# Hybrid recurrent and sparse-attention trunk: a slot table of its own for the first layer

## Chip, cores and metric

The kernel runs on one core of a Trainium2 chip. The metric is the device time of one execution in microseconds (us). The kernel before took 248.72 us (median of 3 runs, 248.48 to 249.34).

## The reference

Two layers, each with one RMS norm, one combined input projection, two mixers in parallel and one output projection onto the residual. The input is 256 tokens of width 1024, all in 32-bit floats.

```python
h = rms_norm(x, norm_g)
z = h @ w_in            # rg_x, rg_gate, q, k_c, v_c, k_s, v_s, k_w, v_w, nsa_gate, br_gate
y_a = rg_lru(causal_depthwise_conv(rg_x, conv_w, conv_b), ...) * silu(rg_gate)
y_b = nsa(q, k_c, v_c, k_s, v_s, k_w, v_w, br_gate, ...) * silu(nsa_gate)
return x + concatenate([y_a, y_b]) @ w_out
```

Mixer A is a gated linear recurrence: two small block products of the convolved rg_x give the gates r and i (tanh forms), from them a decay a and an input u = sqrt(1 - a^2) * i * x, and a scan over the tokens. Mixer B is attention of 8 heads in 2 groups with three branches. The compressed branch turns overlapping blocks of 32 tokens of k_c and v_c through a two-layer network (first product, silu, second product) into 15 keys and values per group; its softmax is small. The selected and the sliding branch cover here the same causal keys. The three are mixed by gates and multiplied by a silu gate.

## The kernel before, in words

Each weight matrix comes in chunks of up to 128 x 1024. A chunk is split into a high part in a rounded format (`wh`) and the rest (`wl`, VectorE, line 170), and each product is three TensorE passes (lines 175 to 177). A layer has 13 chunks ahead of those that matter here (q, keys, compressor input, values), then 12 chunks of 8 x 3 products of 256 columns (function `fm`), which the program calls slots 0 to 11: x0 to x3 (input of the recurrence), n0, n1, g0 to g3, n2, n3 (silu gates of attention and recurrence). Slots 12 to 19 are the output projection (`out_proj`).

The other work of the layer is hung on the slots. The table `SL` says which step stands at which slot, and `at(n, f, ..., mid)` enters it: a step stands ahead of the slot's products, with `mid` after the DMA issues of the slot but still ahead of the products. The loop at the end (lines 842 to 859) writes the program in that order: steps of the slot, loads, casts, mid steps, products, the step that takes up the products (`rg_x`, `rg_gate`, `nsa_gate`), splits of the chunks to come.

That text is not yet the order on the engines. A planner makes one queue per engine out of it: it takes, in a model of the times, the instruction that stands earliest in the text among those whose inputs and buffers are there in the model. On the chip each engine then works through its queue in that fixed order. So a step that is not ready (in the model) is passed by later ones, and a slot's products fill in between.

The steps that the change touches:
- `qk_transpose(t)` (lines 366 to 387): transposes q and k of token block t; copies on ScalarE, rests on VectorE (line 385 writes `qs`), and a copy `qT` (line 387). The second block stands at slot 2 in layer 0, at slot 1 in layer 1.
- The compressor: `cmp_hid` (slot 1), `cmp_act` (slot 2; line 472 writes `hs` on VectorE), `cmp_kv` (second product, lines 477 and 478 on TensorE, a short ScalarE, GpSimd and VectorE chain behind it to line 495), `cmp_kt` (line 499), `cmp_scores` (line 511 and a softmax), `cmp_pt` (line 538).
- Attention for head pair i and token block t: `att_scores` (lines 581 to 583; maximum on VectorE, lines 586 or 588; exponentials on ScalarE, line 594), `att_coef` (ScalarE, line 609), `att_turn` (transposes, line 622, copied out by line 83). `att_out(0)` (lines 636 to 642, slot 7) takes the turned probabilities of head pairs 0 and 1 and the output of `cmp_pt`.
- `rg_gates(j)` (line 665 on TensorE, then lines 668, 669, 671 and 672 on ScalarE), `rg_sqrt` (line 681, ScalarE), `rg_scan` (slot 8).

PSUM banks: the products of `fm` and those of `rg_gates` share two banks (tag "fm"); a bank is free again when its reader has read it: lines 668 and 669 for a gate product, line 654 (VectorE, in `rg_x`) for an x slot, line 544 for a pair of silu slots. Scores have three banks (tag "s"), transposes two ("pp"), the compressor and `att_out` one ("m").

In layer 0 of the kernel before, slot 2 holds `qk_transpose(1)`, `cmp_act`, `att_coef(0,0)` and `rg_gates(0)`; slot 3 holds `cmp_kv`, `att_scores(0,1)`, `att_scores(1,0)`, `att_turn(0,0)` and `rg_gates(1)`, then the products of x3.

Of the kernel before, what the change touches and what calls it, by code (L numbers as in the profile page):

```python
# [38 lines left out]
for _n, _w in (("g", 8), ("cw", 16), ("cb", 4), ("br", 4), ("bi", 4), ("lam", 4)):  # L39
# [12 lines left out]
K = dict(scale="A", ev1="A", hid="A", pct="A")  # L52
SL = dict(qk=(0, 2), order=("x0", "x1", "x2", "x3", "n0", "n1", "g0", "g1", "g2", "g3", "n2", "n3"),
          cmp=(2, 3, 4), att=(1, 3, 3, 4, 6, 7, 10, 11), turn=(3, 4, 5, 6, 8, 10,
          12, 13), cs=(5, 5), cpt=6, aout=(7, 15), gates=(2, 3, 4, 5), tab=6, sqrt=5,
          scan=8, rout=(9, 11))

# [12 lines left out]
def hybrid_trunk_kernel(ctx: ExitStack, tc: tile.TileContext, vx, wc, wt, wv, wf, wo, w1, w2, pe,  # L72
# [185 lines left out]
    def layer(l, prev):  # L258
# [4 lines left out]
        def step(chunk, run, after=None, before=(), middle=()):  # L263
            steps.append((chunk, run, after, before, middle))
# [506 lines left out]
             [F(norm_rope, 1)] + ([] if l else [rms2]))  # L771
        step(Chunk(wv[l, 0, :, 3:6], 3, 280), R(tm2, 3, 3))
        step(Chunk(wv[l, 0, :, 6:], 2, 280), R(tm2, 6, 2), v_out)
        order = [(o[0], int(o[1])) for o in SL["order"]]
        base = {"x": 0, "g": 4, "n": 8}
        post = {"x": rg_x, "g": rg_gate, "n": nsa_gate}
        plan = [([], []) for _ in range(16)]
# [1 line left out]
        def at(n, f, *a, mid=False):  # L779
            plan[n][1 if mid else 0].append(F(f, *a))  # L780

        at(1, cmp_hid)
        at(SL["qk"][0], qk_transpose, 0)
        at(SL["qk"][1] - l, qk_transpose, 1)
        for n, f in zip(SL["cmp"], (cmp_act, cmp_kv, cmp_kt)):
            at(n, f)
        for q in range(8):
            i, t = divmod(q, 2)
            n = SL["att"][q]
            at(n, att_scores, i, t)  # L790
            if q == 0:
                at(SL["qk"][1] - l, att_coef, i, t, mid=bool(l))
            else:
                at(n, att_coef, i, t, mid=True)
        at(SL["cs"][0], cmp_scores)
        at(SL["cpt"], cmp_pt)
        for q in range(8):
            at(SL["turn"][q], att_turn, *divmod(q, 2))
        for i in range(4):
            if i < 2:  # L800
                at(SL["aout"][i], att_out, i)
            at(SL["gates"][i], rg_gates, i)
        at(SL["tab"], next_gains, mid=True)
        at(SL["sqrt"], rg_sqrt, mid=True)
        at(SL["scan"], rg_scan, mid=True)
        for i in range(2):
            at(SL["rout"][i], rg_out, 2 * i, mid=True)
        for n, (kind, j) in enumerate(order):
            c = Chunk(wf[l, base[kind] + j], KT, P, dma=n >= 4)

# [13 lines left out]
    for l in range(DEPTH):  # L824
        prev, st_ = layer(l, prev)
        prev0 = prev0 or prev
        steps += st_
# [140 lines left out]
```

## Time and profile before

| | |
|---|---|
| median of 3 runs | 248.72 us (248.48 to 249.34) |
| the profiled execution | 248.43 us, of which the span of its instructions 246.6 us |
| TensorE busy | 240.6 us (98%), weight loads 222.2 us (90%) |
| VectorE, ScalarE, GpSimd busy | 195.6, 163.8, 38.8 us |
| granted TensorE clock | 0.9 or more in all 40 slices of the page |
| DMA | 57.17 MB, 232 GB/s mean |

The span leaves 1.8 us of the execution outside the instructions. Busy shares overlap: an engine that is busy may be ahead of or behind the one that sets the end. A matmul row gives a start and a modelled end; since matmuls are pipelined, the cost of one is read from the distance between two starts (0.12 us for a product of 256 columns in a run of them).

### The profile page before, as it was taken

The numbers are of one execution on the slowest core, as the hardware profiler recorded it, in microseconds if no ns is written. First come the engines' busy times: TensorE is split into PE (matmuls) and PEld (weight loads), VectorE is DVE, ScalarE is ACT, GpSimd is POOL, SyncE is SP. The second block draws the span as 40 slices with busy tenths as digits, with TensorE's granted clock in tenths as the row PEclk, the third lists the DMA queues.
The fourth block names the chain that finished last, engine by engine and source line by source line (L and its number), as shares of the span: only waits on it lengthen the run. The fifth ranks groups of instructions, "written<-read, shape, count | busy, mean of one in ns | idle before, by whom it ended". The sixth has DMA issues, their size and how long they took to land.

```text
span 246.6 us, 5201 instructions
## 1 busy us (share of the span) xinstructions
PE 240.6 (98%) x1958; PEld 222.2 (90%) x1958; DVE 195.6 (79%) x379; ACT 163.8 (66%) x414; POOL 38.8 (16%) x65
## 2 busy tenths in 40 slices
PE   8999999989999999999999999999999999999994
PEld 3989998978998899979999999987899979998993
DVE  5997897999999988555995569699997999865322
ACT  6965529799999878523863453778999998760100
POOL 0035450012600011000001044101100101110000
PEclk9999999999999999999999999999999999999999
DMA  6988999774789388851479878558559675870022
GB/s 219 358 296 267 347 412 406 258 237 144 248 321 403 116 287 309 244 167 48 144 227 350 306 237 255 182 170 241 193 187 346 229 258 159 292 229 6 3 85 85
DMA packets 17593, 57.17 MB, mean 232 GB/s; under 512 B 2208, under 2 KB 3360, under 8 KB 17056
## 3 DMA queue, kind: packets, MB, share of 16 engines
q1 hardware_dynamic: 12816, 39.86, 46.8%
q0 software_dynamic: 4608, 16.78, 21.5%
q8 instruction: 15, 0.25, 0.4%
q10 hardware_dynamic: 144, 0.20, 0.2%
q14 instruction: 10, 0.08, 0.1%
HBM read 55.78 MB, written 1.05 MB: 230 GB/s over the span
## 4 chain that ended last, share of the span: by engine, by line
PE 81%; DVE 10%; ACT 4%; issue 2%; DMA 1%; DVEq 0%; ACTq 0%
PE fm L175 14%; PE fm L177 13%; PE fm L176 13%; PE pp L622 4%; PE s L176 4%; PE s L177 4%; PE s L175 4%; PE m L636 3%; DVE wl L170 2%; PE s L582 2%; PE s L581 2%; PE fm L665 2%; DVE qs L385 2%; PE pp L177 2%; PE pp L176 2%
## 5 line engine op out<-in xcount | busy, mean ns | idle before, releaser
L170 DVE TENSOR_TENSOR wl<-raw,wh 128x1024 fp32r<-128x1024 f32 (+4 forms) x67 | 74.3, 1114 | 7.8 <-PE pp L176 2.9
L175 PE MATMUL fm<-hh,wh 128*128 128x256 f32 x192 | 56.9, 296 | 0.1
L177 PE MATMUL fm<-hh,wl 128*128 128x256 f32 x192 | 54.7, 285 | 0.0
L176 PE MATMUL fm<-hl,wh 128*128 128x256 f32 x192 | 54.6, 285 | 0.0
L167 ACT CAST wh<-raw 128x768 fp32r<-128x768 f32 (+4 forms) x34 | 30.4, 898 | 26.3 <-DMA raw<-in_wc_dram 6.8
L175 PEld LDWEIGHTS fm<-hh,wh 128*128 128x128 f32 x192 | 36.7, 191 | 1.9 <-issue 1.2
L176 PEld LDWEIGHTS fm<-hl,wh 128*128 128x128 f32 x192 | 36.7, 191 | 0.2
L177 PEld LDWEIGHTS fm<-hh,wl 128*128 128x128 f32 x192 | 36.7, 191 | 0.2 <-DVE wl L170 0.2
L594 ACT ACTIVATE pr<-s,sm 128x128 f32<-128x128 f32 (+1 forms) x64 | 26.2, 424 | 2.7 <-DVE sm L588 1.9
L175 PE MATMUL fm<-yy,wh 128*128 128x256 f32 x96 | 27.4, 285 | 0.0
L176 PE MATMUL fm<-yy,wh 128*128 128x256 f32 x96 | 26.8, 279 | 0.0
L177 PE MATMUL fm<-yy,wl 128*128 128x256 f32 x96 | 26.8, 279 | 0.0
L609 ACT ACTIVATE pr<-pr,sm 128x128 f32<-128x128 f32 (+1 forms) x64 | 23.9, 458 | 2.3 <-DVE sm L600 2.3
L175 PEld LDWEIGHTS fm<-yy,wh 128*128 128x128 f32 x96 | 18.0, 188 | 0.8 <-issue 0.8
L156 POOL DMA_DIRECT2D wh<-in_wo_dram x16 | 8.4, 527 | 62.7 <-PE fm L177 28.0
L176 PEld LDWEIGHTS fm<-yy,wh 128*128 128x128 f32 x96 | 18.1, 188 | 0.0
L177 PEld LDWEIGHTS fm<-yy,wl 128*128 128x128 f32 x96 | 18.0, 188 | 0.0
L156 POOL DMA_DIRECT2D wh<-in_wf_dram x16 | 9.0, 563 | 49.7 <-PE fm L177 17.0
L176 PE MATMUL s<-wl,hh 128*128 128x384 f32 x48 | 16.5, 344 | 0.3 <-DVE wl L170 0.3
L177 PE MATMUL s<-wh,hl 128*128 128x384 f32 x48 | 16.2, 337 | 0.0
L175 PE MATMUL s<-wh,hh 128*128 128x384 f32 x48 | 15.5, 346 | 0.0
L731 DVE TENSOR_TENSOR head<-head,fm 128x512 f32<-128x512 f32 x11 | 7.5, 686 | 9.7 <-PE fm L177 9.6
(206 smaller groups left out, 612.6 us busy)
## 6 DMA issues: line engine op xcount, KB each, us to landing
raw<-in_wf_dram SPq DMA_DIRECT2D x24, 512.0 KB, 4.9
wh<-in_wf_dram POOLq DMA_DIRECT2D x16, 512.0 KB, 4.9
raw<-in_wo_dram SPq DMA_DIRECT2D x16, 512.0 KB, 5.3
wh<-in_wo_dram POOLq DMA_DIRECT2D x16, 512.0 KB, 5.0
raw<-in_wt_dram SPq DMA_DIRECT2D x15, 384.0 KB, 4.1
yy<-in_w_dram SPq DMA_DIRECT2D x4, 1024.0 KB, 7.0
raw<-in_wc_dram SPq DMA_DIRECT2D x4, 512.0 KB, 4.8
raw<-in_wv_dram SPq DMA_DIRECT2D x4, 420.0 KB, 4.6
```

The lines of the kernel that those rows point to most:

```text
L156: G.dma_start(self.wh, self.src)
L167: A.copy(hi[:, c], self.raw[:, c])
L170: V.tensor_tensor(lo[:, c], self.raw[:, c], hi[:, c].bitcast(F32), op=ALU.subtract)
L175: T.matmul(o, lh, rh, start=start, stop=False)
L176: T.matmul(o, lh, rl, start=False, stop=False)
L177: T.matmul(o, ll, rh, start=False, stop=stop)
L385: L.qk_done[t] = V.tensor_tensor(L.qs[HD:, g::2, tok], src, L.qs[:HD, g::2, tok].bitcast(F32), op=ALU.subtract)
L594: A.activation(pr[g][:, b], ov[:, b], AF.Exp, bias=sm[:, 0, 2 * g + b:2 * g + b + 1], accum_out=sm[:, 1, 2 * g + b:2 * g + b + 1])
L609: A.activation(pr[g][:, b], pr[g][:, b], AF.Copy, scale=sc_)
L622: T.transpose(pp[:, (2 * g + b) * P:(2 * g + b + 1) * P], pr[g][:, b, c * P:(c + 1) * P], ident)
L636: T.matmul(o[g * HD:(g + 1) * HD], L.vv[:, 0, b, g * HD:(g + 1) * HD], pt[:, g, b, 0:2].rearrange("p a s -> p (a s)"), start=h == b == 0, ...
L731: V.tensor_tensor(x_sb[:, m], x_sb[:, m], os_[0].rearrange("p (a s) -> p a s", a=2), op=ALU.add)
```

## The change

The first layer gets a table of its own, `SL0`; the second keeps `SL`. The second entry of `cs`, which nothing used, is dropped. In layer 0 the steps move as follows; in layer 1 nothing moves.

| step | slot before | slot after |
|---|---|---|
| `cmp_kv`, `cmp_kt` | 3, 4 | 4, 5 |
| `att_scores` and `att_coef` (0,1), (1,0), (1,1) | 3, 3, 4 | 4, 4, 5 |
| `att_turn` (0,1), (1,0), (1,1) | 4, 5, 6 | 5, 6, 7 |
| `cmp_scores`, `cmp_pt` | 5, 6 | 6, 7 |
| `rg_gates` 1, 2, 3 | 3, 4, 5 | 4, 5, 6 |
| `rg_sqrt` | 5 | 6 |

`att_turn(0,0)` stays at slot 3 and `att_out(0)` at slot 7; the steps of head pairs 2 and 3, `rg_scan` and the rest stay too. No instruction is added or removed.

```diff
--- before.py
+++ after.py
@@ -52,8 +52,12 @@
 K = dict(scale="A", ev1="A", hid="A", pct="A")
 SL = dict(qk=(0, 2), order=("x0", "x1", "x2", "x3", "n0", "n1", "g0", "g1", "g2", "g3", "n2", "n3"),
           cmp=(2, 3, 4), att=(1, 3, 3, 4, 6, 7, 10, 11), turn=(3, 4, 5, 6, 8, 10,
-          12, 13), cs=(5, 5), cpt=6, aout=(7, 15), gates=(2, 3, 4, 5), tab=6, sqrt=5,
+          12, 13), cs=5, cpt=6, aout=(7, 15), gates=(2, 3, 4, 5), tab=6, sqrt=5,
           scan=8, rout=(9, 11))
+
+
+SL0 = dict(SL, cmp=(2, 4, 5), att=(1, 4, 4, 5, 6, 7, 10, 11), turn=(3, 5, 6, 7, 8, 10, 12, 13), cs=6, cpt=7,
+           gates=(2, 4, 5, 6), sqrt=6)
 
 
 
@@ -771,7 +775,8 @@
              [F(norm_rope, 1)] + ([] if l else [rms2]))
         step(Chunk(wv[l, 0, :, 3:6], 3, 280), R(tm2, 3, 3))
         step(Chunk(wv[l, 0, :, 6:], 2, 280), R(tm2, 6, 2), v_out)
-        order = [(o[0], int(o[1])) for o in SL["order"]]
+        S_ = SL if l else SL0
+        order = [(o[0], int(o[1])) for o in S_["order"]]
         base = {"x": 0, "g": 4, "n": 8}
         post = {"x": rg_x, "g": rg_gate, "n": nsa_gate}
         plan = [([], []) for _ in range(16)]
@@ -780,31 +785,31 @@
             plan[n][1 if mid else 0].append(F(f, *a))
 
         at(1, cmp_hid)
-        at(SL["qk"][0], qk_transpose, 0)
-        at(SL["qk"][1] - l, qk_transpose, 1)
-        for n, f in zip(SL["cmp"], (cmp_act, cmp_kv, cmp_kt)):
+        at(S_["qk"][0], qk_transpose, 0)
+        at(S_["qk"][1] - l, qk_transpose, 1)
+        for n, f in zip(S_["cmp"], (cmp_act, cmp_kv, cmp_kt)):
             at(n, f)
         for q in range(8):
             i, t = divmod(q, 2)
-            n = SL["att"][q]
+            n = S_["att"][q]
             at(n, att_scores, i, t)
             if q == 0:
-                at(SL["qk"][1] - l, att_coef, i, t, mid=bool(l))
+                at(S_["qk"][1] - l, att_coef, i, t, mid=bool(l))
             else:
                 at(n, att_coef, i, t, mid=True)
-        at(SL["cs"][0], cmp_scores)
-        at(SL["cpt"], cmp_pt)
+        at(S_["cs"], cmp_scores)
+        at(S_["cpt"], cmp_pt)
         for q in range(8):
-            at(SL["turn"][q], att_turn, *divmod(q, 2))
+            at(S_["turn"][q], att_turn, *divmod(q, 2))
         for i in range(4):
             if i < 2:
-                at(SL["aout"][i], att_out, i)
-            at(SL["gates"][i], rg_gates, i)
-        at(SL["tab"], next_gains, mid=True)
-        at(SL["sqrt"], rg_sqrt, mid=True)
-        at(SL["scan"], rg_scan, mid=True)
+                at(S_["aout"][i], att_out, i)
+            at(S_["gates"][i], rg_gates, i)
+        at(S_["tab"], next_gains, mid=True)
+        at(S_["sqrt"], rg_sqrt, mid=True)
+        at(S_["scan"], rg_scan, mid=True)
         for i in range(2):
-            at(SL["rout"][i], rg_out, 2 * i, mid=True)
+            at(S_["rout"][i], rg_out, 2 * i, mid=True)
         for n, (kind, j) in enumerate(order):
             c = Chunk(wf[l, base[kind] + j], KT, P, dma=n >= 4)
```

## Rows read from the trace of the kernel before

**Rows 1.** Waits of PE: who for whom, us in total, times, longest.

```profile
...
PE m L477 <- DVE hs L472: 0.8, 1, 0.8
...
```

**Rows 2.** Windows of the slots: us, busy per engine, PEclk, DMA share, GB/s.

```profile
51.00:54.00 3.00, 2.15 (x14) 1.31 (x14) 2.77 (x5) 2.98 (x11) 0.54 (x1) 1.00 0.34 91
54.00:84.00 30.00, 30.00 (x246) 26.56 (x246) 29.43 (x61) 29.91 (x88) 7.39 (x14) 1.00 0.72 253
```

**Rows 3.** Timeline of PE around slot 3: start us, us, instruction [idle <-releaser].

```profile
51.18 0.40 PE L581 MATMUL s<-kd,qs 128*128 128x512 f32 x1
52.42 0.30 PE L477 MATMUL m<-w2s,hs 128*32 128x64 f32 x2 [0.85 <-DVE hs L472]
...
52.89 0.48 PE L582 MATMUL s<-kl,qs 128*128 128x512 f32 x1
...
53.26 0.48 PE L581 MATMUL s<-kd,qs 128*128 128x512 f32 x1
53.57 0.40 PE L582 MATMUL s<-kl,qs 128*128 128x512 f32 x1
...
54.66 0.60 PE L622 MATMUL pp<-cst,pr 128*128 128x128 f32 x4
55.10 1.03 PE L665 MATMUL fm<-cx,rws 128*128 128x256 f32 x4
55.78 0.47 PE L175 MATMUL fm<-hh,wh 128*128 128x256 f32 x1
```

**Rows 4.** Timeline of ACT in the same stretch.

```profile
51.13 1.28 ACT L609 ACTIVATE pr<-pr,sm 128x128 f32<-128x128 f32 x4
52.43 0.59 ACT L387 COPY qT<-pp 128x512 f32<-128x512 f32 x1
52.91 0.48 ACT L669 ACTIVATE tmp<-fm,hb 128x256 f32<-128x256 f32 x1
...
56.31 0.46 ACT L668 ACTIVATE rr<-fm,hb 128x256 f32<-128x256 f32 x1
...
58.16 0.46 ACT L594 ACTIVATE pr<-s,sm 128x256 f32<-128x256 f32 x1
```

**Rows 5.** Timeline of DVE in the same stretch.

```profile
51.32 0.69 DVE L385 TENSOR_TENSOR qs<-pp,qs 64x512 fp32r<-64x512 f32 x1
52.05 0.32 DVE L472 SCALAR_TENSOR_TENSOR hs<-hth,m 128x160 f32<-128x160 f32 x1
...
53.42 0.42 DVE L654 TENSOR_TENSOR xpad<-fm,rb 128x256 f32<-128x256 f32 x1
```

**Rows 6.** Timeline of PE: transposes inside the products of slot 4.

```profile
61.61 0.28 PE L175 MATMUL fm<-hh,wh 128*128 128x256 f32 x1
61.73 0.38 PE L622 MATMUL pp<-cst,pr 128*128 128x128 f32 x2
61.86 0.36 PE L176 MATMUL fm<-hl,wh 128*128 128x256 f32 x1
62.07 0.28 PE L177 MATMUL fm<-hh,wl 128*128 128x256 f32 x1
```

**Rows 7.** Windows: slot 0 to the output projection, layer 0, then layer 1.

```profile
37.05:97.75 60.70, 59.85 (x529) 54.13 (x527) 56.32 (x110) 55.42 (x160) 10.60 (x21) 1.00 0.79 273
155.52:215.67 60.15, 59.98 (x529) 53.92 (x527) 53.62 (x109) 53.83 (x158) 6.43 (x13) 1.00 0.69 223
```

**Rows 8.** Timeline of ACT: last read of the fourth gate product.

```profile
71.45 0.46 ACT L669 ACTIVATE tmp<-fm,hb 128x256 f32<-128x256 f32 x1
```

**Rows 9.** Timeline of PE: first product of g0.

```profile
72.22 0.28 PE L175 MATMUL fm<-hh,wh 128*128 128x256 f32 x1
```

**Rows 10.** Timeline of ACT: the table load and the square root.

```profile
75.70 1.28 ACT L681 ACT_TABLE_LOAD   x1
76.99 1.06 ACT L681 ACTIVATE tl<-tl 128x1024 f32<-128x1024 f32 x1
```

**Rows 11.** Line 594 within 60 to 90 us: the load back.

```profile
L594 ACT ACT_TABLE_LOAD  x1: 1283/1283/1283, 80.5 to 80.5; - x1
```

## Prediction

> **What bounds the kernel now.** The page's first part comes first (the table above): TensorE is busy almost throughout. A busy share alone can flatter a pipelined engine, so the second view is that of the waits, for TensorE alone: in the stretch that the change touches there is one wait, 0.8 us of the first product of `cmp_kv` (line 477) for `hs` from VectorE [rows 1]. The third view, busy time by stretch, shows the same: TensorE has 2.15 of 3.00 us in 51 to 54, and 30.00 of 30.00 in 54 to 84, with the clock at 1.00 throughout [rows 2]. In that long stretch ScalarE has 29.91 and VectorE 29.43 of 30.00, so both are full as well. The timelines of the three engines around slot 3 [rows 3 to 5] say why TensorE waits: it is through with slot 2 at 51.18, while ScalarE and VectorE are still at the second block of q and k.
>
> So there is little to win. The whole gap of slot 3 is 0.85 us idle, or 0.93 by starts (51.18 to 52.42, less the 0.31 of one score product of 512 columns, 53.26 to 53.57) [rows 3]. Layer 1, whose second block is transposed a slot earlier, has no such gap; from slot 0 to the output projection it takes 60.15 us, layer 0 takes 60.70, with 529 TensorE rows each [rows 7]. That is 0.55 less. The best case of the change lies between 0.55 and 0.93 us.
>
> **The change part by part.** No instruction comes or goes, and the moved steps issue no DMA, so the sum is one of waits and of order. Three loads for layer 1 (`w2s`, the gain table, the gate weights) hang on the last reads of moved steps; they get later by about a slot and have until layer 1, whose slots begin at 155.52 [rows 7]. The GpSimd power in `cmp_kv` goes behind one more cast trigger; GpSimd is busy 0.54 of 3.00 and 7.39 of 30.00 us in the two stretches [rows 2], so it finds the engine free. I cost both at nothing.
>
> *Slot 3, what TensorE does at 51.18.* The text now has there only `att_turn(0,0)` and the products of x3; `cmp_kv` and the scores come after. Moving them doesn't forbid the planner to take them early, as it did with the score product at 51.18, ahead of `cmp_kv`, which stands before it in the text. The question is what is ready in the planner's model at that moment.
> - `att_turn(0,0)` needs the four scalings of line 609, and of each only its own (transposes of another block go out in pairs between products [rows 6]). On ScalarE `qT` (line 387) comes behind all four although it stands earlier in the text: in the model it became ready only during the fourth, with line 385 [rows 4, 5]. And `hs` follows line 385 on VectorE; it was not ready at 51.18 in the model, but was one score product later. Put together, two or three scalings are over in the model at that moment. So the transposes now come first.
> - On the chip the scalings run from 51.13 to 52.41 [rows 4]. With a release lag of 0.05 (`hs` ends at 52.37, line 477 starts at 52.42 [rows 3, 5]) the fourth transpose starts at 52.46 and, at 0.11 each (54.66 to 55.10 for four), TensorE is free at 52.57. In 1.39 us it has done 0.44 us of work: 0.95 us of waiting, or 0.64 if one score product slips between the third and fourth transpose.
> - `cmp_kv` follows at 52.57 without a wait and costs 0.47 (52.42 to 52.89 [rows 3]), to 53.04. Then the earliest text is x3, but it needs a bank of `fm`. The one of gate product 0 is free when line 669 ends, 53.39; that of x2 when line 654 ends, 53.84 [rows 4, 5]. With the lag, x3 starts at 53.44 (today 55.78 [rows 3]). The 0.40 us between hold a score product (0.31), which leaves 0.09 of waiting; at worst nothing fits (0.40).
> - Waiting in all: 0.95 + 0.09 = 1.04, against 0.93 now: **+0.11 us**. The ends: 0.64 with the 0.40 filled entirely, that is -0.29; and 0.95 + 0.40 = 1.35, that is +0.42. I take +0.11, since its parts follow the order that the three timelines show.
>
> *Slots 4 to 7.* The products of x3 go ahead of most of the scores, of `rg_gates(1)` and the rest, which follow at about 56.3 (53.44 and 24 products of 0.12, 61.61 to 61.73 [rows 6]). TensorE's work is the same; as the stretch is full [rows 2], a changed order costs only where a wait or a break opens. Breaks: a product right behind transposes takes 0.21 (61.86 to 62.07 [rows 6]) in place of 0.12, so 0.09 each. Slot 4 has four such breaks, of which the first is shown; with the turns a slot later there may be none or eight: -0.36 to +0.36, and I take 0, since the scalings that they follow move with them.
>
> *Cover that goes.* Today ScalarE does the four functions of `rg_gates(1)` from 56.31 to 58.16 [rows 4]. These now wait for TensorE to be through with x3, so up to 1.85 us of ScalarE can run empty in a stretch where it is full until 84. What TensorE would feel is late banks: that for g0 is free at 71.91 (line 669, 71.45 + 0.46 [rows 8]), and g0 starts at 72.22 [rows 9], a slack of 0.31. But there is other work to put ahead of g0: `cmp_scores`, a turn and the scores of (2,1) stand in slots 6 and 7 now. I take 0, with an upper end of 1.85 - 0.31 = 1.54. `att_out(0)`, now in the same slot as the `cmp_pt` and the turn it needs, can be passed by products of g1 and g2 and is in the same bound.
>
> *The square root.* `rg_sqrt` moves a slot on, and its table load of 1.28 us [rows 10] is followed by one of 1.28 us back at the next exponential [rows 11]. If it stays between the same two groups of exponentials, the pair stays one, and I cost it at nothing. The Trainium skill, page "ScalarE: Activation LUTs", section "What ACT_TABLE_LOAD costs", puts a switch at 1.28 us for the load and 1.38 for a drain, 2.66 in all. The trace agrees on the load; no drain shows, as the square root starts at 76.99, 0.01 after the load ends [rows 10]. By the page a second pair would cost ScalarE 5.3 us.
>
> *Sum.* 248.43 us (span 246.6 and 1.8 around it) + 0.11 + 0 + 0 = 248.54. The median of the runs is 0.29 above that execution, which would give 248.83; two of the four known times (248.43 and 248.48) lie low, and I forecast **248.6 us**.
>
> **The rivals.** What a measurement here can tell from no change is about 0.3%, 0.75 us.
> 1. *The gap closes.* The planner puts the scores of (0,1) and (1,0) first. One group of (0,1) and all of (1,0) take 1.40 us (53.26 to 54.66 [rows 3]), more than the 1.24 us to be filled. For it: these scores' inputs are there early. Against it: the text has the transposes first, and they are ready in the model. Gain 0.55 to 0.93: 247.5 to 247.9, at best 247.5.
> 2. *ScalarE becomes the bound (slower).* Place: the `fm` bank of g0, or the copies ahead of `att_out(0)`. It starts to cost when ScalarE's lag exceeds 0.31 us; half of the 1.85 gives +0.62, all of it +1.54: 249.1 to 250.0. For it: ScalarE and VectorE are full to 84 [rows 2], and three gate products share two banks with one slot less. Against: the planner sees ScalarE's queue in its model too, and fills with whatever TensorE work is ready.
> 3. *The change does not do what it says.* The planner fills the gap with the same instructions in the same order, the score product and `cmp_kv`, as x3 cannot start before its bank. Then 248.4.
> 4. *A second pair of table loads.* If the square root falls between exponentials of one score block, ScalarE loses 2.57 us more, and by the slack of 0.31 TensorE up to 2.26: 250.7. Against it: the square root waits for the last gates, which don't get earlier.
>
> **How the numbers follow.** Forecast 0.44 (0.38 within 0.3%, 0.03 to either side for the breaks), rival 1 0.22 (0.17 faster, 0.05 too small to tell), rival 2 0.18 (0.16 slower, 0.02 too small), rival 3 0.12 (all within), rival 4 0.04 (slower). Faster 0.03 + 0.17 = 0.20; same 0.38 + 0.05 + 0.02 + 0.12 = 0.57; slower 0.03 + 0.16 + 0.04 = 0.23. The range 247.5 to 250.0 holds rival 1 but for its best end and rival 2 but for its worst; it leaves out some 0.17. The forecast's own range, from the ends of slot 3 and the breaks together, is 247.8 to 249.2 (248.43 - 0.29 - 0.36, 248.43 + 0.42 + 0.36).
>
> **What would show it.** Right: after the last product of x2 TensorE's next rows are line 622, waiting on ScalarE's line 609 for 0.6 to 1.0 us in all; line 477 has no wait; x3 begins at 53.4 to 53.6 with most of the scores behind it; 54 to 84 stays full for TensorE; ScalarE shows a gap near 56; there are two table loads around one square root in layer 0; layer 1 still takes 60.15 us from slot 0 to its output projection. Wrong: score rows before line 622 and no wait at all in slot 3 (rival 1), idle TensorE before g0 or ahead of `att_out(0)` (rival 2), line 477 still waiting (rival 3), a third or fourth load (rival 4). If layer 1 or the stretch before 51 us changed by more than 0.3 us, the frame of the argument would be wrong.

## The result and the profile after

The kernel after took 250.49 us (median of 4 runs, 250.34 to 250.78); the kernel before took 248.66 us in the same series (median of 4, 248.48 to 249.34). The ratio is 1.0063, with a 95% interval of 1.0042 to 1.0084. On 248.8 us that is +1.57 us (1.04 to 2.09): slower, with an interval that lies clear of no change. The forecast was 248.6 us, with a chance of 0.57 on no change; the time lies 0.5 us above the range, whose upper end was 250.0. The profiled execution took 250.34 us, of which the span is 248.6.

Lines of the kernel after are those of before plus 4 (line 477 is now 481, 622 is 626, 636 is 640, 83 is 87).

First the waits of TensorE (who for whom, us in total, times, longest), which answer to [rows 1].

```profile
PE m L117 <- DVE wz L114: 1.1, 1, 1.1
PE fm L181 <- DVE wl L174: 0.6, 1, 0.6
PE pp L626 <- ACT pt L87: 0.5, 1, 0.5
```

The wait for `hs` is gone, as the change's order promised. The first line, 1.1 us, lies at the start of the program and is in the kernel before too. The other two are new. That for `wl` lies in slot 0, ahead of everything that moved; more on it below. The last is the one to remember: transposes that wait for a copy of ScalarE.

Next TensorE's timeline around slot 3, against [rows 3], and at two places far behind it (start us, us, instruction; xN is a row of N).

```profile
51.50 0.28 PE L181 MATMUL fm<-hh,wl 128*128 128x256 f32 x1
51.64 1.20 PE L626 MATMUL pp<-cst,pr 128*128 128x128 f32 x4
52.78 0.30 PE L481 MATMUL m<-w2s,hs 128*32 128x64 f32 x2
...
53.25 0.48 PE L585 MATMUL s<-kd,qs 128*128 128x512 f32 x1
53.57 0.32 PE L179 MATMUL fm<-hh,wh 128*128 128x256 f32 x1
...
85.79 0.47 PE L585 MATMUL s<-kd,qs 128*128 128x512 f32 x1
86.20 0.65 PE L640 MATMUL m<-pt,vv 128*64 128x256 f32 x4
...
89.81 1.09 PE L626 MATMUL pp<-cst,pr 128*128 128x128 f32 x8
90.66 0.47 PE L586 MATMUL s<-kl,qs 128*128 128x512 f32 x1
91.60 0.66 PE L626 MATMUL pp<-cst,pr 128*128 128x128 f32 x4 [0.47 <-ACT pt L87]
92.01 0.37 PE L179 MATMUL fm<-hh,wh 128*128 128x256 f32 x1
...
99.69 0.28 PE L179 MATMUL fm<-yy,wh 128*128 128x256 f32 x1
99.90 0.65 PE L640 MATMUL m<-pt,vv 128*64 128x256 f32 x2
100.48 0.39 PE L179 MATMUL fm<-yy,wh 128*128 128x256 f32 x1
```

The reader is to see three places here. At 51.64 to 53.57 slot 3 runs as forecast. At 89.81 to 92.01, ahead of n2, the last four of twelve transposes wait: the score product of line 586 is followed by line 626 after 0.94 us (90.66 to 91.60), where such a product takes 0.24 elsewhere (91.63 to 91.87 in e2 below). At 99.90 one pair of products of `att_out(1)` (a row of x2) stands alone among the output projection's products.

ScalarE's timeline, against [rows 4, 10, 11], shows where the delay comes from.

```profile
51.19 1.28 ACT L613 ACTIVATE pr<-pr,sm 128x128 f32<-128x128 f32 x4
...
55.40 0.19 ACT L486 ACTIVATION_READ_ACCUMULATOR kq<-m 32x1 f32 x1
...
57.13 0.60 ACT L659 ACTIVATE cx<-xpad,head 128x256 f32<-128x256 f32 x1 [1.55 <-DVE xpad L658]
58.17 0.47 ACT L598 ACTIVATE pr<-s,sm 128x256 f32<-128x256 f32 x1 [0.44 <-DVE sm L590]
...
75.35 0.37 ACT L518 COPY tmp<-m 128x256 f32<-128x256 f32 x1
...
80.14 1.28 ACT L685 ACT_TABLE_LOAD   x1
81.44 1.06 ACT L685 ACTIVATE tl<-tl 128x1024 f32<-128x1024 f32 x1
82.52 1.28 ACT L598 ACT_TABLE_LOAD   x1
...
85.62 0.38 ACT L87 COPY pct<-m 128x256 f32<-128x256 f32 x1
85.88 1.10 ACT L87 COPY pt<-pp 128x512 f32<-128x512 f32 x2
...
88.34 1.69 ACT L613 ACTIVATE pr<-pr,sm 128x256 f32<-128x256 f32 x4
...
90.97 0.58 ACT L87 COPY pt<-pp 128x512 f32<-128x512 f32 x1
```

ScalarE is idle for 1.55 and 0.44 us between 55 and 59, where it used to do the functions of `rg_gates(1)`. From there on the compressor is late: its copy of line 518 is at 75.35 (before: 68.16), and the copy of `cmp_pt`'s output, which `att_out(0)` needs, is at 85.62 (before: 77.96). The copies of the turned probabilities of (1,1) stand right behind it, at 85.88 (before: 78.21).

Last the windows: the two of [rows 2], then slot 0 to the output projection in layer 0 and in layer 1 [rows 7].

```profile
51.00:54.00 3.00, 3.00 (x20) 2.17 (x19) 2.94 (x6) 2.98 (x9) 0.54 (x1) 1.00 0.40 130
54.00:84.00 30.00, 30.00 (x232) 26.93 (x231) 26.84 (x56) 27.41 (x78) 9.42 (x15) 1.00 0.86 282
...
37.05:98.92 61.87, 60.84 (x528) 54.03 (x526) 55.68 (x107) 55.48 (x160) 12.11 (x21) 1.00 0.79 264
157.46:217.61 60.15, 59.99 (x528) 53.93 (x527) 53.62 (x109) 53.92 (x158) 6.43 (x13) 1.00 0.69 222
```

ScalarE fell from 29.91 to 27.41 us busy in 54 to 84, and VectorE from 29.43 to 26.84; that work is done later. TensorE's busy time stays at 30.00 and shows nothing of it. Note that 51 to 54 now shows 3.00 of 3.00 although 0.70 us of it is waiting: a row of four transposes that start 0.29 us apart counts as one stretch of work. Only the starts tell.

**Where the time went.** Starts of the same products in the two traces, after less before. The stretch from x3 counts in before from 53.33, the moment at which it has done as much work as after has at 53.57 (52.89 [rows 3] and 0.44 for the four transposes).

| stretch of TensorE | before | after | difference |
|---|---|---|---|
| start of the span to the last product of x2 (same queue) | | | +0.45 |
| slot 3, x2's end to equal progress | 2.15 | 1.93 | -0.22 |
| from there to the output projection | 44.42 | 45.34 | +0.92 |
| output chunks 0 to 3 | 15.97 | 16.76 | +0.79 |
| from there to the end | | | 0.00 |

The sum, +1.94, is the whole difference at the start of layer 1 (155.52 and 157.46); the two profiled executions differ by 1.91.

The first two rows belong together. What TensorE waits for in slot 3 of the kernel after are ScalarE's scalings of `att_coef(0,0)`, and these start almost at the same time in both traces: 51.13 [rows 4] and 51.19. Counted from them, equal progress is 2.20 us on in before and 2.38 in after. A second trace of the queue of before (f1 below) and one of a kernel with the order of after in slot 3 (e1 below) have the scalings at these times:

```profile
51.92 1.28 ACT L613 ACTIVATE pr<-pr,sm 128x128 f32<-128x128 f32 x4
...
51.37 1.28 ACT L613 ACTIVATE pr<-pr,sm 128x128 f32<-128x128 f32 x4
```

From there to equal progress f1 takes 2.20 again, and e1, e2, e4 and f2 take 2.38 each. So the new order of slot 3 costs 0.18 us, and the late end of x2 adds nothing to it, since TensorE then only waits less. The -0.22 of the table is therefore no gain of the change. From the scalings on, the trace of after has lost 0.18, 0.92 and 0.79, some 1.9 us, against the +1.57 (1.04 to 2.09) over the runs.

Of the +0.92 the wait ahead of n2 is 0.70; the rest, 0.22, is put down to breaks in the order, without a row for each. The +0.79 is the lone pair. In before the whole of `att_out(1)` stands in one piece:

```profile
107.00 0.27 PE L177 MATMUL fm<-yy,wl 128*128 128x256 f32 x1
107.20 0.65 PE L636 MATMUL m<-pt,vv 128*64 128x256 f32 x4
...
110.81 0.38 PE L175 MATMUL fm<-yy,wh 128*128 128x256 f32 x1
```

In after the rest of `att_out(1)`, without the pair, takes as long later (108.94 to 112.76, 3.82) as the whole did before (107.00 to 110.81, 3.81).

### The profile page after: what moved, and what is told of

The parts are those of the page before. It is cut to its first block, busy times and chain, and to the rows that moved or that the text cites. A ratio compares the mean times of both kernels' runs of the same rounds, so it can differ in the third digit from the quotient of the medians.

```text
span 248.6 us, 5204 instructions
## 1 busy us (share of the span) xinstructions
PE 242.7 (98%) x1958; PEld 223.6 (90%) x1958; DVE 195.4 (79%) x379; ACT 164.3 (66%) x414; POOL 41.8 (17%) x65
## 4 chain that ended last, share of the span: by engine, by line
PE 75%; DVE 10%; DMA 4%; POOL 4%; ACT 3%; issue 2%; SPq 1%; DVEq 0%; ACTq 0%; POOLq 0%
PE fm L179 14%; PE fm L181 13%; PE fm L180 13%; PE pp L626 4%; PE s L179 3%; PE s L181 3%; PE s L180 3%; DVE wl L174 2%; PE fm L669 2%; PE m L640 2%; DMA ga<-in_gains_dram 2%; PE s L585 2%; PE s L586 2%; DMA raw<-in_wt_dram 2%; PE s L587 1%
## 5 line engine op out<-in xcount | busy, mean ns | idle before, releaser
L626 PE MATMUL pp<-cst,pr 128*128 128x128 f32 x96 | 15.3, 278 | 0.5 <-ACT pt L87 0.5
```

Source lines behind the costliest of these rows:

```text
L626: T.transpose(pp[:, (2 * g + b) * P:(2 * g + b + 1) * P], pr[g][:, b, c * P:(c + 1) * P], ident)
```

## Experiments

All are edits of the kernel after. My theory (A) was that two places far behind the moved steps carry the loss, the wait ahead of n2 and the lone pair of `att_out(1)`, and that slot 3 and the late compressor as such cost next to nothing. The rivals were that the late compressor carries it alone, that a single group of the moved steps does, or that the new table in itself does something else. The table gives each run's ratio with its 95% interval; "us" is the ratio's share of 248.8. The next two columns are TensorE's stretches of the table above, 44.42 and 15.97 in before; the first is left out where slot 3 has another order. The last column is a difference to before in one trace each: the time from the start of ScalarE's scalings in slot 2 (line 609) to layer 1's slot 0, which is 104.39 us in before (51.13 to 155.52). It leaves out what comes ahead of the moved steps, and all but f3 have it within the interval of their runs.

| kernel | median | ratio | us | x3 to output | chunks 0 to 3 | scalings to layer 1 |
|---|---|---|---|---|---|---|
| after | 250.49 | 1.0063 [1.0042, 1.0084] | +1.57 | 45.34 | 16.76 | +1.88 |
| e1_pin | 249.91 | 1.0044 [1.0027, 1.0062] | +1.09 | 45.34 | 15.98 | +1.10 |
| e2_turn11 | 249.81 | 1.0037 [1.0017, 1.0057] | +0.92 | 44.66 | 16.26 | +0.70 |
| e3_gates_only | 249.77 | 1.0029 [1.0017, 1.0041] | +0.72 | | 16.99 | +1.01 |
| e4_cmp_back | 250.96 | 1.0078 [1.0061, 1.0095] | +1.94 | 44.34 | 17.84 | +1.97 |
| f1_null | 248.73 | 0.9999 [0.9983, 1.0015] | -0.02 | 44.41 | 15.98 | -0.01 |
| f2_pin_cmp_back | 249.51 | 1.0025 [1.0013, 1.0037] | +0.62 | 44.33 | 16.64 | +0.70 |
| f3_kv_only | 249.92 | 1.0042 [1.0028, 1.0057] | +1.04 | | 15.98 | +0.64 |
| f4_kv_turn | 249.54 | 1.0036 [1.0023, 1.0049] | +0.90 | | 15.98 | +0.81 |

**e1_pin.** The first products of `att_out(1)` may not go out ahead of the last product of the third output chunk; all else as in after.

```diff
+ L.op_last = mm3(...)        # in out_proj; mm3 returns its last product
...
+ with tc.issue_after(L.op_last.ins) if l == 0 and u == 1 else nullcontext():
      T.matmul(o[g * HD:(g + 1) * HD], L.vv[:, 0, b, g * HD:(g + 1) * HD], ...
```

> The changed kernel, with the first products of att_out(1) in layer 0 tied behind the last product of the third output chunk; all else in the queues stays in its order (three products of the second half of the output projection fill the place). Theory A, the loss is in how the planner now orders the late slots: in the changed kernel's trace one product of att_out(1) stands alone between products of the output projection at 99.90 and costs about 0.77 us with the switches around it, while the rest of att_out(1) takes as long as all of it did before. Without it: 250.49 - 0.77 = 249.7. Theory B, ScalarE's lag is the bound (rival 2 of the prediction): where that one product stands does not matter, 250.5. Theory C, the wait of 0.56 us in slot 0 ahead of everything that was moved: 250.5, and the wait is seen again.

The output chunks fell from 16.76 to 15.98 us, which is before's 15.97, and nothing else moved (45.34). Over the runs 0.47 us came back. The intervals of the two ratios overlap, so the trace carries this verdict more than the time does. There is no wait in slot 0 in this trace, so theory C, that this wait carries the loss, falls.

**e2_turn11.** `att_turn(2,1)` one slot later.

```diff
- turn=(3, 5, 6, 7, 8, 10, 12, 13)
+ turn=(3, 5, 6, 7, 8, 11, 12, 13)
```

> The changed kernel, with att_turn(2,1) hung on slot 11 in place of 10. In the queue the twelve transposes in a row ahead of the products of n2 become six and the others come a slot later, and att_out(1) is whole again. Theory A: the wait of TensorE for the copy ahead of n2 (0.7 us by starts) and the lone product (0.77) both go: 249.0. Theory B, ScalarE's lag: the copies are as late as before and something else waits, 250.0 to 250.5. Theory C, slot 0: 250.5.

TensorE ahead of n2:

```profile
90.54 0.66 PE L626 MATMUL pp<-cst,pr 128*128 128x128 f32 x4
90.95 0.48 PE L586 MATMUL s<-kl,qs 128*128 128x512 f32 x1
...
91.63 0.40 PE L586 MATMUL s<-kl,qs 128*128 128x512 f32 x1
91.87 0.28 PE L587 MATMUL s<-maskb,identb 128*128 128x256 bf16 x1
91.99 0.38 PE L626 MATMUL pp<-cst,pr 128*128 128x128 f32 x2
92.12 0.36 PE L179 MATMUL fm<-hh,wh 128*128 128x256 f32 x1
```

The run of twelve transposes is broken, a score group stands between, and no wait is left: 0.68 us less from x3 to the output projection. In the planner's new order there is no lone pair either, but one transpose of head pair 3 stands alone among the output products (100.18): 16.26 in place of 15.97. Only 0.65 us of the expected 1.5 came back over the runs. The trace has +0.53 left behind x3, which with the 0.18 of slot 3 makes 0.71; the runs have +0.92 (0.42 to 1.42).

**e3_gates_only.** Only `rg_gates` and `rg_sqrt` are moved.

```diff
+ SL0 = dict(SL, gates=(2, 4, 5, 6), sqrt=6)
```

> Of the change only rg_gates 1 to 3 and rg_sqrt move a slot on. In the queue att_out(0) stands in the products of g1 as before, att_out(1) is whole, and no run of transposes is longer than before. Theory A: no loss, 248.4 to 249.0. Theory B, gate products squeezed into two banks and ScalarE late: slower, 249.3 to 250.2, with a wait ahead of g0.

Theory A missed: slower, though neither of my two places occurs. The time falls into theory B's range, but there is no wait ahead of g0. The trace has a third place, at the end of the first output chunk. TensorE, VectorE and ScalarE there:

```profile
101.43 0.28 PE L181 MATMUL fm<-yy,wl 128*128 128x256 f32 x1
101.86 1.52 PE L626 MATMUL pp<-cst,pr 128*128 128x128 f32 x6
...
99.82 0.18 DVE L603 RECIPROCAL sm<-sm 128x4 f32<-128x4 f32 x1
99.92 1.21 DVE L174 TENSOR_TENSOR wl<-raw,wh 128x1024 fp32r<-128x1024 f32 x1
101.04 0.15 DVE L604 TENSOR_TENSOR sm<-gate,sm 128x4 f32<-128x4 f32 x1
...
101.29 1.71 ACT L613 ACTIVATE pr<-pr,sm 128x256 f32<-128x256 f32 x4 [0.50 <-DVE sm L604]
```

A weight split of 1.21 us got between the reciprocal and the small product of `att_coef(3,1)` on VectorE; so the scalings start 0.50 late and the transposes crawl. TensorE is about 1.0 us later behind this chunk than ahead of it.

**e4_cmp_back.** `cmp_scores` and `cmp_pt` back at slots 5 and 6, the rest as in after.

```diff
- cs=6, cpt=7,
```

> The changed kernel with cmp_scores and cmp_pt back at slots 5 and 6. In the queue att_out(0) stands in the products of g1 again (in two pieces), and the run of twelve transposes is gone; but att_out(1) is cut into four pieces between products of the output projection. Theory A, as pieces cost: no wait ahead of n2 (-0.7), three or four lone pieces at 0.3 to 0.77 each in place of one: 249.8 to 251.5. Theory D, the late compressor output alone makes the loss: 248.7 to 249.0. Theory B: 250.0 to 250.5.

This takes the late compressor away, and with it the wait ahead of n2 (44.34, as before's 44.42), and yet the kernel is slower than after: `att_out(1)` now goes out in four pieces among the output chunks, which take 17.84, as theory A had it. The rival that the late compressor alone is the loss falls.

**f1_null.** The new table holds the old slots.

```diff
+ SL0 = dict(SL)
```

> The new table filled with the old values: the queues of the kernel before. Theory A: ratio 1.000 within 0.002; a wait of 0 to 1.2 us for wl in slot 0 comes and goes from execution to execution, with the same queue, and what it delays is taken back at slot 3, where ScalarE and VectorE set the time. Theory C, that this wait belongs to the change: no such wait here, in any case.

It measures as the kernel before, with the wait for `hs` back (0.8 us). So the second table as such does nothing. The other half of theory A did not show: the wait in slot 0 is 0.06 us here, and although x2 ends 0.80 us later than in before, slot 3 takes nothing of it back, since ScalarE's scalings are as late (0.79).

**f2_pin_cmp_back.** e4 with the tie of e1.

> The changed kernel with cmp_scores and cmp_pt back at slots 5 and 6 (as in the run that took 250.96) and, in addition, the first products of att_out(1) tied behind the third output chunk. Theory A: the pieces of att_out(1) cost 1.87 us in that run's trace (17.84 us from the first output product to that of the fifth chunk, 15.97 in the kernel before), so 250.96 - 1.87 = 249.1. Theory B, ScalarE's lag: unchanged, 251.0.

It takes back 1.3 us of e4, of 1.87 expected. The chunks take 16.64: five transposes stand singly among the first output products, as in e4. This has the lowest ratio of the versions with moved steps, still +0.62 us, though its interval and that of e3 overlap.

**f3_kv_only.** Only `cmp_kv` a slot later, `cmp_kt` left where it was.

```diff
+ SL0 = dict(SL, cmp=(2, 4, 4))
```

> Of the change only cmp_kv moves to slot 4 (cmp_kt stays there). In the queue the four score products of (0,1) and (1,0) now stand ahead of the transposes in slot 3 and cmp_kv after the products of x3; att_out(0) and att_out(1) are whole. This is rival 1 of the prediction brought about. If the gap of slot 3 is worth what was said: 248.66 - 0.55 to 0.93, that is 247.7 to 248.1, no wait in slot 3. If a later place gives it back: 248.5 to 249.5, and the trace shows where.

This is rival 1 brought about: scores fill slot 3 (52.28 to 54.21 without a gap), and no product waits for `hs`. Then slot 4:

```profile
60.21 0.69 PE L669 MATMUL fm<-cx,rws 128*128 128x256 f32 x2
61.09 0.44 PE L626 MATMUL pp<-cst,pr 128*128 128x128 f32 x2 [0.18 <-ACT pr L613]
61.36 0.60 PE L669 MATMUL fm<-cx,rws 128*128 128x256 f32 x2
61.97 0.44 PE L626 MATMUL pp<-cst,pr 128*128 128x128 f32 x2
```

TensorE came earlier and waits here for ScalarE's scalings instead: two gate products take 0.88 (60.21 to 61.09) and the next two 0.61, where before had the four in a row in 0.68 (60.39 to 61.07). So most of the gain is given back within 8 us, and the kernel ends +1.04, slower than either outcome expected. The trace places only 0.64 of that; the rest is open.

**f4_kv_turn.** f3 with `att_turn(0,0)` at slot 4 as well.

```diff
+ SL0 = dict(SL, cmp=(2, 4, 4), turn=(4, 4, 5, 6, 8, 10, 12, 13))
```

> As the last, and att_turn(0,0) moves to slot 4 too, so that slot 3 has scores and gates ahead of x3 and no transposes that wait for ScalarE. Rival 1: 247.7 to 248.1. If later places give it back: 248.5 to 249.5.

Not to be told from f3, and not better than before: 0.04 us above the range expected. Behind x2 its waits are small and in three places (0.15, 0.17 and 0.31 us).

## Why the prediction was wrong, and where it was right

- *What bounds the kernel.* Right: TensorE's stream sets the end. Of the 0.93 us to be won, at most, no version won any. Layer 1 still takes 60.15 us.
- *Slot 3.* Right in order and size. Line 626 comes first and waits, line 481 has no wait, one score product fits, x3 starts at 53.57 (forecast 53.4 to 53.6). The cost, counted from ScalarE's scalings, is +0.18 in all five traces with this order, against a forecast of +0.11 with ends -0.29 and +0.42. The waiting is 0.70 in after, where x2 ended late, and 1.10 in e1 and f2, where it did not (forecast 1.04).
- *The square root.* Right: one pair of loads around one root in layer 0. The root starts 0.02 us after its load ends (80.14 and 1.28, then 81.44). The drain of 1.38 us that the Trainium skill names (page "ScalarE: Activation LUTs", section "What ACT_TABLE_LOAD costs") does not show after either.
- *Cover that goes.* The size on ScalarE was nearly right: 1.99 us idle between 55 and 59, a little over the upper end of 1.85. The price on TensorE was the step that failed: "I take 0", because `att_out(0)` can be passed by products of g1 and g2. It was passed, by g1, g2 and g3 (86.20 in place of 78.60). But passing is not free of what stands behind the one that is passed. In both kernels the transposes of (2,0) follow `att_out(0)`. In before that left 6.9 us from the first of them to the first of (2,1):

```profile
82.67 0.60 PE L622 MATMUL pp<-cst,pr 128*128 128x128 f32 x4
...
89.58 1.04 PE L622 MATMUL pp<-cst,pr 128*128 128x128 f32 x8
```

In after TensorE is through with `att_out(0)` at 89.81, when the scalings of (2,1) are all but through (88.34 and 1.69). So all twelve transposes stand in one run on two banks; the third group of four needs the bank of the first, whose copy on ScalarE stands behind exponentials and starts at 90.97, and TensorE waits 0.70 us ahead of n2. Why (2,0) could not go earlier is not shown by a run: its step is later in the text, both "pt" buffers (line 621 of after) belong to head pairs 0 and 1 until `att_out(0)` has read them, and both "pp" banks hold (1,1), turned at 75.06 and 76.44, until the two copies at 85.88. Nor is it the compressor alone that makes `att_out(0)` late: in e4, with the compressor back, its first half starts at 77.81, but the second, which needs (1,1), at 87.08. Rival 2 had the mechanism, a late ScalarE, and one of the places, the copies ahead of `att_out(0)`; but TensorE had other products there, g0 started at 72.00 without a wait, and the price came behind.

- *Slots 4 to 7.* The same step in its other half: "a changed order costs only where a wait or a break opens", with the window drawn at slot 7. The planner settles the order with what is ready in its model, and a changed state at slot 7 changes its choices up to the output projection, 45 us behind the moved steps. There it put a pair of products of `att_out(1)` ahead of the rest (presumably into a gap of the model, which no run shows), and that costs 0.79 us. The forecast priced breaks of 0.09 in four places of slot 4 and none there.
- *The sum.* The terms forecast at nothing measured +0.92 and +0.79; e1 takes the second away, e2 the first and most of the second, e4 and f2 exchange them for others. What no trace places is 0.22 us behind x3 in after, and 0.40 in f3.
- *The signs.* All that were to show it right came true, and the forecast was wrong all the same: in layer 0 they look no further than 84 us, and the losses lie at 91 and 99. The sign for a wrong frame, a change of more than 0.3 us ahead of 51, came true as well (+0.45), but it is a difference that two executions of one queue show too (0.80 in f1).

Not settled: why the compressor's copy on ScalarE comes 7.2 us later where its scores come only 3.95 later (69.04 against 65.09). A third "pt" buffer or a third "pp" bank, which might let the turns pass `att_out(0)`, was not tried.

## What to carry to other kernels

Where a planner writes the queues and the bound engine is full, a moved step is priced by the whole queue that comes out, not by the slots that it leaves and enters: list the bound engine's order up to the next point where all versions agree, and look at what stands right behind a step that is passed. A gap on the bound engine is worth little if the two engines beside it have 29.4 and 29.9 of 30 us to do: in f3 most of it was given back a few microseconds on. All eight kernels here with moved steps were slower than before, by 0.25 to 0.78%, whether the gap of 0.93 us closed or not.

## What the runs showed of the hardware

- The wait in slot 0 for a split weight (line 174 for line 181) comes and goes. Up to x2 all these kernels have the same queues on TensorE and VectorE, and the wait is 0 in before, e1, f2 and f4, 0.06 in f1, about 0.55 in after, e3 and e4, 0.81 in f3 and 1.15 in e2. So moved steps do not need to bring it (e1, f2, f4); why five of the eight kernels with moved steps have it and both traces of the old order do not is open. One profiled execution against another can differ by a microsecond there. The first thing to do with two traces is to find where their queues part, and the next to count from the engine that is waited for there: five traces with one order in slot 3 take 1.93 to 2.33 us of TensorE from the end of x2, but 2.38 each from ScalarE's scalings.
- A lone pair of half-column products among the output projection's costs far more than its share. It is 0.58 us from its start to the next product's (99.90 to 100.48), 0.09 more ahead of it (99.69 to 99.90, in place of 0.12) and 0.10 behind it (100.48 to 100.70), 0.77 in all. Its two products start 0.27 us apart (99.90 and 100.17). The whole of `att_out(1)`, 40 such products in a run, took 3.61 before (107.20 to 110.81), 0.18 a pair.
